# A tuned encoder layer: weight sums in DRAM given out in another order

## The chip, the cores and the metric

The kernel runs on one core of one Trainium2 chip. The metric is the device time of one execution in microseconds (us). Three runs of the kernel before took 811.58, 812.87 and 814.30 us; their median is 812.87 us. The core has a matmul engine (TensorE, PE in the profile), a vector engine (VectorE, DVE), a scalar engine (ScalarE, ACT), GpSimd (POOL) and SyncE (SP). They run on their own and wait for one another through semaphores. Transfers between DRAM and on-chip memory go over 16 DMA engines; in this kernel SP issues the loads, and POOL issues the transfers that add to what is at their target.

## The reference

One layer of a streaming encoder over 512 frames with 1024 channels, in float32:

```python
u = rmsnorm(h, g_mix)
proj = u @ w_in      # GLA q,k,v,out-gate,low rank | FoX q,k,v,forget | memory query | 3 branch gates
# branch A: gated linear attention in chunks of 64 frames, normed, times silu(out-gate), @ w_gla_o
# branch B: forgetting attention (8 heads, causal), @ w_fox_o
# branch C: cross attention into rmsnorm(mem) @ w_mem_kv (4 heads), @ w_mem_o
gt = sigmoid(gates)
merged = gt[0] * y_gla + gt[1] * y_fox + gt[2] * y_mem
h = h + merged @ w_out
u2 = rmsnorm(h, g_ffn)
h = h + square(relu(u2 @ w_ff1)) @ w_ff2
out = rmsnorm(h, g_final)
```

The large products are u by w_in (1024 by 6680), merged by w_out, and the feed-forward block (1024 by 4096 and back).

## The kernel before, in words

**Products.** Every float32 weight chunk of 512 KB is loaded into a tile `raw`, and *split*: ScalarE casts it to a shortened float type (`hi`, or `whi`), VectorE subtracts that from the load (`lo`, or `wlo`). Three products, hi by hi, hi by lo and lo by hi, then make one (`mm3`, L186 to L188). The ring of `raw` tiles has three buffers, and so have the rings of `hi` and `lo`: a load starts when the third split before it is done.

**Seven products instead of eight.** The GLA value and out-gate columns of w_in, the branch gates and w_ff1 and w_ff2 are multiplied in 2 by 2 blocks by a scheme that needs seven block products and, in return, sums of blocks. Sums of activations are made by VectorE. Sums of weights are made by DMA: a transfer copies a block in DRAM to a scratch tensor in DRAM, and later ones, issued by POOL, add other blocks to it. The scratch tensors are G1 to G4 for the GLA columns (`gsum`, 1 MB each) and T1 to T4 for w_ff1 (`tsum`). The ff block runs over four quarters of w_ff1. The first quarter has tensors of 512 KB (T1 to T4, in two halves, numbered 0 and 4); each of the later quarters, 1 to 3, has T1 and T3 of 1 MB. The gates' sums are made in on-chip memory instead (`wb`, L1211, POOL too), and so are most later ones of the ff block (`b`, L1855, and `tq`, L1572).

**What sets the pace of the sums in DRAM.** `next_sum` (L136) is called at every split, from `split_w` (L173) and, in the gate products, from `high` (L1222). After the first seven splits it takes the next entry of a list, if there is one, and issues that transfer on POOL so that it waits for the cast of this split. An add waits, besides, for the transfer that wrote its target before. There are two lists: `first_ops()` (G1 to G4, then the first quarter's T1 to T4, then T3 of quarters 1 to 3), and T1 of quarters 1 to 3. `late_on` switches from the first to the second, in the round that is named (2, 7) before. The second list's transfers also wait for the last merge of the second branch.

**Order.** The program is written by stages, which overlap: the front (memory keys and values, norm of x); FoX attention, woven with projections and with GLA products 1, 5, 2 and 6 (`linear`, L552); memory attention, woven with the FoX output product and GLA products 7 and 3; GLA, woven with its product 4 and the memory branch's output; then *rounds*, a list of block products of the three branch gates with the merge, `("Y", ...)` for the GLA output product and `("O", ...)` for half of the product with w_out (L1417 to L1440); then the other half of w_out, the second norm and the ff block. PE's order is the written one. The other engines' order inside most stages is set by a scheduler that simulates the program; in the rounds and a few other places it is the written one (`in_order`). All engines take their instructions in order, so one that waits holds back all behind it.

GLA product 4 (`linear(4, A22r)`) reads G4, the ff block's first quarter T4, T3 and the others, and the second quarter T1 and T3 of quarter 1. PE reads a sum only by way of a load and a split.

Of the kernel before, what the change touches and what calls it, by code (L numbers as in the profile page):

```python
# [58 lines left out]
def hybrid_block(ctx, tc, chunks, wst, memT, xT, xN, gffn, gfin, wup, cst, out):  # L59
# [16 lines left out]
    def pool(name, side=None, bufs=1):  # L76
        return tc.tile_pool(name=name, bufs=bufs, side=side, reuse_waits="tile")
# [32 lines left out]
    def linear_ops():  # L110
        for n, src, add in ((1, "11", 0), (3, "12", 0), (1, "12", 1), (2, 1, 0), (2, "22", 1), (3, "22", 1), (4, 2, 0), (4, "21", 1)):
            if isinstance(src, str):
                i = index["N", "w_in", 4 * (src[0] == "2"), OFF["gv" if src[1] == "2" else "gg"]]
                src = wst[i:i + 2]
            else:
                src = gsum[src]
            yield gsum[n], src, add

    def sum_ops(ops, qs):
        for n, src, add in ops:  # L120
            for q in qs:
                i = index["F", q % 4, 0 if q else 1, src] if isinstance(src, str) else None
                yield tsum[n, q], tsum[src, q] if i is None else wst[i:i + (2 if 0 < q < 4 else 1)], add

    def first_ops():
        lin = linear_ops()
        ff = sum_ops(((1, "11", 0), (3, "12", 0), (1, "12", 1), (3, "22", 1), (2, 1, 0), (2, "22", 1), (4, 2, 0), (4, "21", 1)), (0, 4))
        for own, others in ((4, 1), (1, 3), (1, 1), (1, 1), (1, 0)):
            yield from islice(lin, own)
            yield from islice(ff, others)  # L130
        yield from ff
        yield from sum_ops(((3, "12", 0), (3, "22", 1)), (1, 2, 3))

    sums = [first_ops(), sum_ops(((1, "11", 0), (1, "12", 1)), (1, 2, 3))]
    late_on, merged = [], [None]
    chunk_n, cast_now, low_now, hold = [0], [None], [None], [None]  # L136

    def next_sum(after):

        chunk_n[0] += 1  # L140
        if chunk_n[0] <= 7:
            return
        for to, src, add_ in islice(sums[len(late_on)], 1):
            with tc.issue_after(merged[0]) if late_on else ExitStack():
                if add_:
                    d = nc.gpsimd.dma_start(to, src, accum_op=ALU.add, max_dma_last_dim=8192)
                else:
                    d = nc.gpsimd.dma_start(to, src)
            tc.add_manual_dep(d.ins, after.name, mybir.DependencyInfo(mybir.DependencyClass.Sync, mybir.DependencyReason.DATA),
                              reason="pace")  # L150

    @contextmanager
    def in_order(*others):

        engines = (mybir.EngineType.DVE, mybir.EngineType.Activation, mybir.EngineType.SP, *others)
        traced = nc.cur_bb.bb.instructions
        last, behind = traced[-1], {}
        yield
        for i in traced[next(k for k in reversed(range(len(traced))) if traced[k] is last) + 1:]:
            if i.engine in engines:  # L160
                if i.engine in behind:
                    tc.add_manual_dep(i, behind[i.engine].name, mybir.DependencyInfo(
                        mybir.DependencyClass.NoSync, mybir.DependencyReason.DATA), reason="order")
                behind[i.engine] = i
# [53 lines left out]
    def run(*gens):  # L218
        for g in gens:
            for _ in g:  # L220
                pass
# [391 lines left out]
    with pool("fox") as xp:  # L613
# [242 lines left out]
        T, V_, R, A, K = fox_turn, fox_values, fox_rows, fox_scores, fox_masks  # L856
# [54 lines left out]
    with pool("mematt") as ap:  # L911
# [3 lines left out]
        def mem_q(h):  # L915
            def evac(ps):
                st["q", h] = [ap.tile([P, S], F32R, tag=g, name=nm(g), bufs=2) for g in ("qh", "ql")]
                st["low"] = split(*st["q", h], ps)
            return proj(OFF["mq"] + P * h, evac)
# [44 lines left out]
        Q, A, T, V_ = (lambda i: run(mem_q(i))), mem_scores, mem_turn, mem_values  # L964
# [183 lines left out]
    def h_tile(t, name):  # L1148
        return hp.tile([P, D], F32, tag=f"h{t}", name=nm(name))
# [18 lines left out]
    with pool("outp") as op_:  # L1168
# [38 lines left out]
        def load_sum(g, n, other):  # L1207
            nc.sync.dma_start(sum_tile(g, n, other), wst[index[gate_key(GATES[g], "12" if other else "11", n)]])

        def plus(g, n, other, b):  # L1210
            nc.gpsimd.dma_start(sum_tile(g, n, other), wst[index[gate_key(GATES[g], b, n)]], accum_op=ALU.add)  # L1211
# [10 lines left out]
        def high(r, c):  # L1222
            ws[r, c] = pair_tiles()
            next_sum(nc.scalar.copy(ws[r, c][0], source(r, c)).ins)  # L1224

        def low(r, c):
            hi, lo = ws[r, c]
            nc.vector.tensor_tensor(lo, source(r, c), f(hi), op=ALU.subtract)  # L1228
            if r[0] not in ("Y", "O") and r[1] in (1, 5, 6) and r != (0, 1):
                plus(r[0], c, 0, {1: "12", 5: "22", 6: "21"}[r[1]])  # L1230
# [30 lines left out]
        def bend():  # L1261
            for x, to in bent:
                nc.scalar.activation(x, x, AF.Tanh, scale=0.5)
                if to[0] < 2:
                    todo.extend((*to, t) for t in range(2))
            bent.clear()
# [36 lines left out]
        def merge(g, i, c, half):  # L1303
            t = 2 * i + half
            x, a = th[g, i, c][:, half], half_of(acc[t], c)
            if g == 0:
                nc.vector.scalar_tensor_tensor(a, x, 1.0, a, op0=ALU.add, op1=ALU.mult)
            else:
                nc.vector.scalar_tensor_tensor(x, x, 1.0, half_of(ymem[t], c), op0=ALU.add, op1=ALU.mult)
                merged[0] = vec(a, a, x)  # L1310
# [56 lines left out]
        def go(when, i):  # L1367
            for fn, args in when.get(i, []):
                fn(*args)
# [5 lines left out]
        with in_order(mybir.EngineType.Pool):  # L1375
            for n in range(2):
                load_sum(0, n, 0)
                plus(0, n, 0, "12")
            go(loads, 0)
            loads[0] = []  # L1380
            for n in range(2):
                load_sum(0, n, 1)
            for i, r in enumerate(rounds):
                now[0] = r
                if r == (2, 7):
                    omst.close()
                    mhp = late.enter_context(pool("mhl"))
                    mh, ml = (mhp.tile([P, KT, S], F32R, name=x) for x in ("mh", "ml"))
                if r == ("Y", 0):
                    hN += [h_tile(t, "h") for t in range(NT)]  # L1390
                    gf = hp.tile([P, D], F32, tag="gf", name="gf")
                    for t in (2, 3, 0, 1):
                        nc.sync.dma_start(hN[t], xN[t * P:(t + 1) * P, :])
                    nc.sync.dma_start(gf, gffn)
                if r == ("O", 0):
                    mst.close()
                    unp.append(late.enter_context(pool("un")))
                go(loads, i)
                go(early, i)
                n = NT if r[0] in ("Y", "O") else 2  # L1400
                parts, due = todo[:1], [(r2, c) for r2 in rounds[i + 1:i + 2] for c in range(2)]
                del todo[:1]
                for x in parts:
                    merge(*x)
                if i:
                    evac(rounds[i - 1], NT - 1 if rounds[i - 1][0] in ("Y", "O") else 1)
                for t in range(n):
                    mms(r, t)
                    if t == 0:
                        for x in due:  # L1410
                            high(*x)
                            low(*x)
                        bend()
                        go(after, i)
                        if r == (2, 7):
                            late_on.append(1)
                    else:  # L1417
                        evac(r, t - 1)
                    if r == ("Y", 0):
                        turn(t, 1)  # L1420
                    if r == ("O", 1):
                        turn(t, 0)
            evac(r, n - 1)
# [761 lines left out]
```

## Time and profile before

| | |
|---|---|
| median of three runs | 812.87 us |
| the profiled execution | 813.05 us |
| its span, first to last instruction | 811.3 us |
| mean granted PE clock | 0.991 of full speed |
| PE busy | 793.0 us, 98% of the span |
| VectorE, ScalarE, POOL busy | 76%, 58%, 12% |
| DMA moved | 165.44 MB, of it 65.02 MB by POOL's queue (q0) and 95.72 MB by SP's (q1) |
| share of the 16 DMA engines | 38.1% by POOL's queue, 32.8% by SP's |
| sums of T from weights | 12 of 512 KB and 6 of 1 MB with sizes shown, and 6 copies |

The profile is of one execution. Times are in us from the start of the span. L176 is line 176 of the kernel before. `raw<-in_wst_dram` reads "raw written from the weights in DRAM". In a row of the timeline stand start, duration, engine, line, operation, output and inputs, and in brackets the idle time of the engine ahead of it with what ended it. In the view of the chain of waits each row is start, duration and what the time went to: a DMA row runs from its issue to the instruction that it released. A row of the DMA view ends with the time from issue to landing. Ends of products are modelled, so the distance between the starts of two products is the better measure.

In the pages' rows the DRAM tensors are just `T` and `G`; in the rows on order they have numbers, where T_0, T_1 to T_3 and T_4 are the ff quarters (0 and 4 the halves of the first), and G_91 to G_94 are G1 to G4. T_0_77 is T1 and T_0_79 is T3 of the first quarter; T_1_82, T_2_84 and T_3_86 are T3 of the other quarters, T_1_81, T_2_83 and T_3_85 are their T1.

### The profile page before, as it was taken

To read this page: it belongs to the slowest core of one execution; us is meant where nothing else is said; L and a number is where in the kernel's file an instruction comes from. 1 tells how busy PE (TensorE), PEld (TensorE's weight loads), DVE (VectorE), ACT (ScalarE), POOL (GpSimd) and SP (SyncE) were. 2 spreads that over 40 slices of the span, in tenths; PEclk is the share of its full clock that TensorE was granted. 3 is DMA by queue.
4 is the path that set the end of the run, shared out by engine and by line. 5 is a ranking of instruction groups with operands and counts; after the bars stand their busy time and mean duration, and the time that the engine had idled before them with its cause. 6 is when DMAs were issued, how large, how long until landed. Compare 5 with 4: busy or idle time off the path is not lost.

```text
span 811.3 us, 11675 instructions
## 1 busy us (share of the span) xinstructions
PE 793.0 (98%) x4351; PEld 678.6 (84%) x4351; DVE 620.3 (76%) x971; ACT 474.2 (58%) x746; POOL 97.4 (12%) x137
## 2 busy tenths in 40 slices
PE   9999999989999999999999999999999999999995
PEld 7788888868888888788887789987998899889975
DVE  6878899756777677667744748788789778987896
ACT  7767566534554465655622546864676467646854
POOL 0001000110110122202110000012001200110011
PEclk9999999999999999999999899999999999999998
DMA  9354766993869469798879515998967986798453
GB/s 356 138 166 170 243 228 182 268 272 108 230 242 258 149 186 232 201 239 199 204 246 308 161 52 198 283 233 216 233 180 189 222 220 178 179 253 228 99 91 117
DMA packets 41577, 165.44 MB, mean 204 GB/s; under 512 B 4944, under 2 KB 5648, under 8 KB 39440
## 3 DMA queue, kind: packets, MB, share of 16 engines
q0 software_dynamic: 12448, 65.02, 38.1%
q1 hardware_dynamic: 27712, 95.72, 32.8%
q10 hardware_dynamic: 1360, 3.96, 1.5%
q8 instruction: 34, 0.56, 0.3%
q14 instruction: 23, 0.19, 0.1%
HBM read 162.55 MB, written 31.49 MB: 239 GB/s over the span
## 4 chain that ended last, share of the span: by engine, by line
PE 84%; DMA 8%; DVE 5%; issue 1%; ACT 1%; SPq 0%; POOLq 0%; DVEq 0%; POOL 0%; ACTq 0%
PE mm L1465 16%; PE mm L186 14%; PE mm L187 14%; PE mm L188 14%; DMA raw<-in_wst_dram 6%; PE a L188 4%; PE a L186 4%; PE a L187 4%; PE mm L1805 3%; PE mm L1806 1%; DMA xt<-in_xT_dram 1%; PE mm L715 1%; DVE wlo L177 1%; PE a L430 1%; DMA mem_s<-in_memT_dram 1%
## 5 line engine op out<-in xcount | busy, mean ns | idle before, releaser
L177 DVE TENSOR_TENSOR wlo<-raw,whi 128x1024 fp32r<-128x1024 f32 x44 | 53.8, 1223 | 35.7 <-ACT whi L176 35.0
L176 ACT CAST whi<-raw 128x1024 fp32r<-128x1024 f32 x44 | 46.2, 1050 | 53.5 <-DMA raw<-in_wst_dram 18.4
L1465 PE MATMUL mm<-u,hi 128*128 128x256 f32 x384 | 64.7, 283 | 0.0
L1465 PEld LDWEIGHTS mm<-u,hi 128*128 128x128 f32 x384 | 56.4, 189 | 0.1
L187 PE MATMUL mm<-lo,ch 128*128 128x512 f32 (+1 forms) x132 | 51.2, 388 | 0.4 <-DVE lo L1525 0.4
L186 PE MATMUL mm<-hi,ch 128*128 128x512 f32 (+1 forms) x132 | 50.9, 386 | 0.0
L188 PE MATMUL mm<-hi,cl 128*128 128x512 f32 (+1 forms) x132 | 50.9, 386 | 0.0
L1524 ACT CAST hi<-raw 128x1024 fp32r<-128x1024 f32 x34 | 35.7, 1051 | 25.8 <-PE mm L1465 12.2
L1525 DVE TENSOR_TENSOR lo<-raw,hi 128x1024 fp32r<-128x1024 f32 x34 | 41.5, 1222 | 10.3 <-ACT hi L1524 10.3
L1855 POOL DMA_DIRECT2D b<-in_wst_dram x30 | 25.7, 855 | 197.6 <-DVE lo L1525 89.6
L1465 PE MATMUL mm<-u,lo 128*128 128x256 f32 x192 | 47.5, 283 | 0.0
L1465 PE MATMUL mm<-u2s,hi 128*128 128x256 f32 x288 | 47.3, 283 | 0.0
L186 PE MATMUL mm<-uhl,whi 128*128 128x512 f32 x112 | 44.6, 399 | 0.0
L188 PE MATMUL mm<-uhl,wlo 128*128 128x512 f32 x112 | 43.9, 392 | 0.1
L187 PE MATMUL mm<-uhl,whi 128*128 128x512 f32 x112 | 43.7, 390 | 0.0
L1524 ACT CAST hi<-b 128x1024 fp32r<-128x1024 f32 x26 | 27.3, 1048 | 25.7 <-PE mm L188 18.4
L1465 PEld LDWEIGHTS mm<-u2s,hi 128*128 128x128 f32 x288 | 41.5, 190 | 0.0
L1525 DVE TENSOR_TENSOR lo<-b,hi 128x1024 fp32r<-128x1024 f32 x26 | 31.7, 1221 | 7.9 <-ACT hi L1524 7.7
L186 PE MATMUL a<-hi,ch 128*128 128x512 f32 (+1 forms) x96 | 37.1, 387 | 0.4 <-DVE h L1518 0.4
L1228 DVE TENSOR_TENSOR lo<-wb,hi 128x1024 fp32r<-128x1024 f32 x21 | 25.3, 1222 | 15.7 <-ACT hi L1224 15.7
L187 PE MATMUL a<-lo,ch 128*128 128x512 f32 (+1 forms) x96 | 37.1, 387 | 0.0
L188 PE MATMUL a<-hi,cl 128*128 128x512 f32 (+1 forms) x96 | 37.0, 385 | 0.0
(531 smaller groups left out, 2393.7 us busy)
## 6 DMA issues: line engine op xcount, KB each, us to landing
raw<-in_wst_dram SPq DMA_DIRECT2D x108, 512.0 KB
b<-in_wst_dram POOLq DMA_DIRECT2D x32, 512.0 KB, 5.6
wb<-in_wst_dram POOLq DMA_DIRECT2D x24, 512.0 KB, 7.6
b<-in_wst_dram SPq DMA_DIRECT2D x16, 512.0 KB
raw<-T SPq DMA_DIRECT2D x14, 512.0 KB
T<-in_wst_dram POOLq DMA_DIRECT2D x12, 512.0 KB, 6.3
T<-in_wst_dram POOLq DMA_DIRECT2D x6, 1024.0 KB, 11.8
wb<-in_wst_dram SPq DMA_DIRECT2D x12, 512.0 KB
```

The costliest lines, as they stand in the source:

```text
L176: cast = nc.scalar.copy(hi, raw)
L177: low_now[0] = nc.vector.tensor_tensor(lo, raw, f(hi), op=ALU.subtract).ins
L186: nc.tensor.matmul(ps, lh, rh, start=start, stop=False, skip_group_check=on)
L187: nc.tensor.matmul(ps, lh, rl, start=False, stop=False, skip_group_check=on)
L188: nc.tensor.matmul(ps, ll, rh, start=False, stop=stop, skip_group_check=on)
L430: nc.tensor.matmul(ps, x[:, k, sl], w[low][:, kk, :], start=k == low == 0 and x is mxh, stop=k == KT - 1 and low == 1)
L1228: nc.vector.tensor_tensor(lo, source(r, c), f(hi), op=ALU.subtract)
L1465: nc.tensor.matmul(ps[:, a, :], x[:, a, k, :], y[:, s, k, :], start=start, stop=stop, skip_group_check=go is not None)
L1524: split_now[0] = nc.scalar.copy(hi, raw).ins
L1525: split_now[1] = nc.vector.tensor_tensor(lo, raw, f(hi), op=ALU.subtract).ins
L1805: nc.tensor.matmul(ps, wh[:, a, k, :], u[:, k], start=k == 0, stop=False, skip_group_check=True)
L1855: nc.gpsimd.dma_start(to[i], wst[index["B", q, i, x]], accum_op=ALU.add)
```

## The change

The entries of `first_ops()` are given out in another order, which is now written as a string with one letter for each split: L is the next entry for the GLA sums, F the next one for the first ff quarter, T the next one for T3 of quarters 1 to 3, and a dash is a split that gives out nothing. The first ten entries are as before. Then come five splits with nothing, where the adds to T1 of the first quarter, the copy and the add for G4, and an add to T3 stood. G4's copy and add follow, alternating with the three 1 MB copies for T3 of quarters 1 to 3; the three 1 MB adds to them come every third entry. What is left of the first quarter (T4) comes last, so that the list is five splits longer and ends within the GLA stage and the first rounds. The second list, T1 of quarters 1 to 3, is switched on in round (2, 4), two rounds later than (2, 7), with one output product between them. No transfer is added, dropped or resized, and no product, cast or load is.

```diff
     def first_ops():
         lin = linear_ops()
         ff = sum_ops(((1, "11", 0), (3, "12", 0), (1, "12", 1), (3, "22", 1), (2, 1, 0), (2, "22", 1), (4, 2, 0), (4, "21", 1)), (0, 4))
-        for own, others in ((4, 1), (1, 3), (1, 1), (1, 1), (1, 0)):
-            yield from islice(lin, own)
-            yield from islice(ff, others)
+        third = sum_ops(((3, "12", 0), (3, "22", 1)), (1, 2, 3))
+        for who in "LLLLFLFFFL-----LTLTTFFTFFTFFT":
+            yield from islice({"L": lin, "F": ff, "T": third}[who], 1) if who != "-" else [None]
         yield from ff
-        yield from sum_ops(((3, "12", 0), (3, "22", 1)), (1, 2, 3))
...
-        for to, src, add_ in islice(sums[len(late_on)], 1):
+        for to, src, add_ in filter(None, islice(sums[len(late_on)], 1)):
...
-                        if r == (2, 7):
+                        if r == (2, 4):
                             late_on.append(1)
```

## The prediction

> **What bounds the kernel now.** I read the page first, then TensorE's (PE's) waits, then a table of stretches, then the chain of waits inside the two stretches where PE loses time. The page's span:
>
> ```profile
> span 811.3 us, 11675 instructions
> ```
>
> The profiled execution took 813.05 us, so 1.75 us lie outside the span; it stands 0.18 us above the median of the runs shown (812.87). PE is busy nearly throughout, so a change of DMA order can only pay where PE waits. The view of PE's waits (total, times, longest, in us) has three that touch this change:
>
> ```profile
> PE a L186 <- ACT mh L1322: 2.6, 1, 2.6
> PE a L186 <- ACT qh L239: 1.9, 1, 1.9
> PE a L188 <- DVE ql L240: 1.0, 1, 1.0
> ```
>
> The table of stretches says where, and what the DMA engines did then (us of each engine with its count, then the granted PE clock, the busy share of the 16 DMA engines, GB/s):
>
> ```profile
> 144.00:183.00 39.00, 35.99 (x171) 29.89 (x170) 24.46 (x31) 17.52 (x26) 6.31 (x9) 0.96 0.98 269
> 205.00:224.00 19.00, 19.00 (x105) 16.37 (x104) 16.54 (x26) 9.90 (x20) 3.42 (x5) 1.00 0.90 260
> 224.00:231.00 7.00, 7.00 (x33) 5.79 (x32) 5.38 (x13) 6.10 (x15) 0.48 (x1) 1.00 0.12 46
> 420.00:445.00 25.00, 25.00 (x127) 20.60 (x126) 10.00 (x14) 4.46 (x7) 1.62 (x2) 1.00 1.02 292
> 445.00:463.00 18.00, 15.25 (x55) 11.74 (x54) 11.37 (x16) 10.92 (x17) 0.00 (x0) 0.81 0.52 172
> 463.00:488.00 25.00, 25.00 (x129) 21.16 (x129) 14.82 (x24) 11.49 (x24) 1.65 (x3) 1.00 0.20 64
> ```
>
> Both gaps end a stretch in which the DMA engines are full (0.98, 1.02), and in both the clock falls (0.96, 0.81). The chain of waits (start, duration) names the late thing, weight loads:
>
> ```profile
> 147.58 14.17 DMA raw<-in_wst_dram
> ...
> 164.17 10.98 DMA raw<-in_wst_dram
> ```
>
> ```profile
> 422.63 23.68 DMA raw<-in_wst_dram
> ```
>
> Why PE feels a late load shows on ScalarE, which runs in order: a cast that waits for its load (the load of 164.17, there at 175.2; the one below) holds back the evacuation that stands behind it, qh in the first gap (A, at 175 us) and mh in the second (B, at 445).
>
> ```profile
> 176.18 0.58 ACT L239 CAST qh<-mm 128x512 fp32r<-128x512 f32 x1
> ```
>
> ```profile
> 445.13 1.04 ACT L1224 CAST hi<-raw 128x1024 fp32r<-128x1024 f32 x1 [11.93 <-DMA raw<-in_wst_dram]
> ```
>
> **Gap A (175 us), the first term.** Price it from PE's own rows: the last product of the second memory query, and the first of the third.
>
> ```profile
> 174.54 0.39 PE L188 MATMUL mm<-uhl,wlo 128*128 128x512 f32 x1
> ...
> 183.79 0.39 PE L186 MATMUL mm<-uhl,whi 128*128 128x512 f32 x1
> ```
>
> Between them stand 12 score products and 12 output products. Undisturbed, 12 score products take 1.43 us (208.12 to 209.55), and a 512-column product follows the last in 0.227 us (459.66 to 462.38 holds 12):
>
> ```profile
> 208.12 0.28 PE L186 MATMUL a<-mkh,qh 128*128 128x256 f32 x1
> ...
> 209.55 0.40 PE L186 MATMUL mm<-whi,s 128*128 128x512 f32 x1
> ```
>
> ```profile
> 459.66 0.39 PE L186 MATMUL a<-hi,mh 128*128 128x512 f32 x1
> ...
> 462.38 0.39 PE L186 MATMUL mm<-f0h,mh 128*128 128x512 f32 x1
> ```
>
> So the third query could start at 174.54 + 0.23 + 1.43 + 12 x 0.227 = 178.92 us and starts at 183.79: A costs 4.9 us, 2.9 of waiting and 2.0 of slow clock.
>
> What the change does there: five casts in a row give out no sum. These are the issues that go, first and last of five:
>
> ```profile
> 146.59 0.79 POOL L146 DMA_DIRECT2D T<-in_wst_dram  x1 [1.35 <-ACT whi L176]
> ...
> 167.06 0.79 POOL L146 DMA_DIRECT2D T<-in_wst_dram  x1 [3.08 <-ACT whi L176]
> ```
>
> They are three adds of 512 KB, one copy of 1 MB and one add of 1 MB. Lone DMAs (issue to landing in us, last number) land in:
>
> ```profile
> T<-in_wst_dram POOLq DMA_DIRECT2D x1, 512.0 KB, 5.5
> ```
>
> ```profile
> T<-T POOLq DMA_DIRECT2D x1, 512.0 KB, 3.8
> ```
>
> ```profile
> T<-in_wst_dram POOLq DMA_DIRECT2D x1, 5.5
> ```
>
> ```profile
> G<-in_wst_dram POOLq DMA_DIRECT2D x1, 1024.0 KB, 8.4
> ```
>
> in order a 512 KB add, a 512 KB copy, a 1 MB copy (its size is not printed) and a 1 MB add. Steps between these rows price the DMA work: another 512 KB of adding is 8.4 - 5.5 = 2.9 us, of copying 5.5 - 3.8 = 1.7. The five are then 5 x 2.9 + 2 x 1.7 = 18 us of DMA time out of a stretch of 39 that is full. To save A, the load that came at 175.2 must come by about 172; the two loads in its chain took 14.17 and 10.98 us. With 18 us of work gone from around them I expect more than these 3. ScalarE's order here is unchanged, and the second-next bound, the cast's target buffer, comes free when PE ends the first query, at about 169 us. **I take the whole 4.9 us**; bounds 0 (the load still later than 175) and 4.9.
>
> **Gap B (445 us), the second term.** Last transposes at 444.78, then the round's 48 products, then the next product at 462.38 (above).
>
> ```profile
> 444.78 0.60 PE L1320 MATMUL mm<-cst_s,acc 128*128 128x128 f32 x4
> ```
>
> Undisturbed: 444.78 + 0.60 + 48 x 0.227 = 456.28, so B costs 6.1 us, 2.6 of waiting and 3.5 of slow clock. The load of 422.63 stood behind five 512 KB loads and these six sums (first and last):
>
> ```profile
> 403.53 0.54 POOL L148 DMA_DIRECT2D T<-in_wst_dram  x1 [11.54 <-ACT hi L1224]
> ...
> 429.82 0.80 POOL L146 DMA_DIRECT2D T<-in_wst_dram  x1 [7.35 <-ACT f0h L1224]
> ```
>
> Three are copies, three adds of 1 MB. T1's list now opens two rounds later, so before the load lands only two copies stay, on the casts at 420 and 428: an add at 415.77 and two at 421.65 and 429.82 leave, 3 x 2 x 2.9 = 17 us of adding, and one copy with them. The load needs to be some 4 us earlier (cast, cast, evacuation before 445.4). **I take the whole 6.1 us**; bounds 0 and 6.1.
>
> Where T1's work goes: its last copy and three adds fall on 436 to 460 us, by the casts of the last product and of its successor. In the table 445 to 463 is half empty and 463 to 488 four fifths; its 6 x 2.9 + 2 x 1.7 = 21 us fit into 18 x 0.48 + 25 x 0.80 = 28.6 us idle. If that cover were gone, the weights for the ff block's first products would come late and each us would be PE's. The sums themselves are read a quarter later. On ScalarE and VectorE, in the same place, two casts and subtractions move behind one evacuation (ACT, where the last product's weights are cast; mh is the merged activation turned for it). Before:
>
> ```order
> 360 L1322 ACTIVATE mh<-mm_4146 128x4x128
> 361 L239 CAST f1h_4261<-raw_4263 128x1024
> 362 L239 CAST f0h_4255<-raw_4257 128x1024
> 363 L176 CAST whi_4269<-raw_4267 128x1024
> 364 L1322 ACTIVATE mh<-mm_4165 128x4x128
> 365 L1155 ACTIVATE hsq_4204,hss_3028<-h_3971 128x512
> ```
>
> of the change:
>
> ```order
> 360 L1321 ACTIVATE mh<-mm_4144 128x4x128
> 361 L238 CAST f0h_4253<-raw_4255 128x1024
> 362 L1321 ACTIVATE mh<-mm_4163 128x4x128
> 363 L238 CAST f1h_4259<-raw_4261 128x1024
> 364 L175 CAST whi_4267<-raw_4265 128x1024
> 365 L1154 ACTIVATE hsq_4202,hss_3028<-h_3967 128x512
> ```
>
> The evacuation comes earlier and the two casts one step later, some 10 us ahead of their products: nothing, with the 48 products as cover. Loads (SP) and products (PE) keep their order.
>
> **Memory stage (205 us), the third term, a loss.** The sums that left 146 to 168 come back here. POOL gives out the sums, one row each (G: the GLA weights' sums; T with a quarter: the ff weights'; 64x2048 is an add of 512 KB, 128x2048 of 1 MB; 16 rows are a copy). From the 1 MB add near 144 us on, before:
>
> ```order
> 23 L146 DMA G_93<-in_wst_dram 128x2048
> 24 L146 DMA T_0_77<-in_wst_dram 64x2048
> 25 L148 DMA G_94<-G_92 16x16384
> 26 L146 DMA T_4_87<-in_wst_dram 64x2048
> 27 L146 DMA G_94<-in_wst_dram 128x2048
> 28 L146 DMA T_0_79<-in_wst_dram 64x2048
> ```
>
> of the change:
>
> ```order
> 24 L147 DMA G_94<-G_92 16x16384
> 25 L147 DMA T_1_82<-in_wst_dram 16x16384
> 26 L145 DMA G_94<-in_wst_dram 128x2048
> 27 L147 DMA T_2_84<-in_wst_dram 16x16384
> 28 L147 DMA T_3_86<-in_wst_dram 16x16384
> 29 L145 DMA T_0_77<-in_wst_dram 64x2048
> 30 L145 DMA T_4_87<-in_wst_dram 64x2048
> 31 L145 DMA T_1_82<-in_wst_dram 128x2048
> ```
>
> G4 and the 1 MB copies of T3 of quarters 1 to 3 have come ahead of the adds for the first ones, each at least a memory-stage cast later than its row's old place. The tight spot is one load and what its cast holds back: the exponentials of the third head (L939), behind which VectorE scales them (L943) and PE turns them (L951).
>
> ```profile
> 213.03 1.05 ACT L176 CAST whi<-raw 128x1024 fp32r<-128x1024 f32 x1 [3.86 <-DMA raw<-in_wst_dram]
> ```
>
> That load meets, in place of an add of 512 KB, a 1 MB copy (5.5 against 5.5 us, no difference) and then, in place of a copy of 512 KB, an add (5.5 - 3.8 = 1.7 more); the next pair is the same again. Later by 0 (it passes before the second DMA) to 3.4 us; a gain is excluded, as PE has no gap to return in that stretch (19.00 of 19.00). A gap of 3.4 would bring a slow spell like B's, 3.5: bounds 0 and 6.9. **I take 1.0 us**, the half of the first pair and a little, without a clock loss. [...] After it, the extra adding (1.7 + 1.7 + 2.9) fills the 6.2 us that 224 to 231 has idle. G4's add now issues near 182 and waits on POOL for G4's copy, two casts before it, with only sums behind; it has until these loads:
>
> ```profile
> 231.51 2.12 SPq L566 DMA_DIRECT2D raw<-G  x2
> ```
>
>
> **GLA stage.** From 231 on there are 512 KB sums where 1 MB ones were, less to move, and five more sums behind them. On POOL they now stand around the powers that the GLA norms need; what could be late is the third power, behind an add that follows the cast at 278.88:
>
> ```profile
> 278.88 1.04 ACT L176 CAST whi<-raw 128x1024 fp32r<-128x1024 f32 x1
> ```
>
> ```profile
> 283.32 1.01 POOL L1107 TENSOR_TENSOR stat<-stat,mhalf 128x4 f32<-128x4 f32 x1 [10.93 <-DVE stat L1106]
> ```
>
> The add would issue at about 280.2 and be off POOL at 281.0, 2.3 us before the power's operand. Nothing; if later, each us goes to the turns behind the norm.
>
> **Sum.** 813.05 - 4.9 - 6.1 + 1.0 = 803.05 us for a profiled execution; 0.18 less for a median of runs: **802.9 us**.
>
> **Rivals.** (1) One cure is lost or given back. For it: ScalarE's blocked order stays as it was, and A's and B's loads still share with 1 MB sums. Against it: both stretches lose 18 us of DMA time and more. Only B cured: 802.9 + 4.9 = 807.8; only A: 809.0; both cured but the full 6.9 at 213 us: 808.8. (2) Only the waits return and the slow spells stay: 812.87 - 1.9 - 1.0 - 2.6 + 1.0 = 808.4. The row against it: the clock is 1.00 in every stretch above but the two with gaps. [...] (3) Slower: the backlog of 144 to 183 moves whole into the memory stage, whose casts block ScalarE in the same way. Price: 18 us of waiting and two slow spells of 3.5, less 11.0: +14, 827 us; it decides where the casts from 213.03 on come over 7.5 us late in sum (7.5 and one spell of 3.5 eat 11.0). Against it: 224 to 231 is idle to 88%. (4) The change does nothing measurable, since gains and new gaps cancel or the loads wait for buffers instead: 812.9.
>
> **Chances.** Forecast (800 to 805.5) 0.70; (1) 0.14; (2) 0.03; (3) 0.05; (4) 0.05; below 800, by a gain that I don't see, 0.03. I call faster what is over 0.3% (2.4 us) below 812.87, about what a measurement of this kernel tells from no change. (1) and (2) are faster: 0.90; same 0.05; slower 0.05. The range goes from 800 (third term 0, and runs 1.3 us under their median, as the fastest shown) to 809 (the bound of the third term, and one cure lost).
>
> **What would show it.** A right: the waits on qh and ql leave PE's list, the clock is 1.00 in 144 to 183, and the third query's first product follows the second's last within 4.5 us, not 9.25. B right: the wait on mh at L1322 is gone and the last product's loads take 12 us, not 23. Third term: a new wait of PE at L951 in the third head's turn, about 1 us. Wrong: a slow clock anywhere between 180 and 300 us, or ScalarE waiting over 5 us for raw there.

## The result, and the profile after

The changed kernel took 800.10, 800.70 and 803.69 us; the ratio to the kernel before, which ran beside it, is 0.986, with a 95% interval of 0.982 to 0.990. (A fourth run took 1595.49 us, of a cause that nothing here shows; the ratio leaves it out.) Four more runs of it, in the experiments, had a median of 803.34 us (801.91 to 807.28) and a ratio of 0.987 (0.983 to 0.991). The forecast was 802.9. The profiled execution took 800.10 us. Its page begins:

```profile
span 798.3 us, 11673 instructions
```

The span is 13.0 us shorter. Line numbers are one less than in the kernel before. The view of PE's waits no longer has qh, ql or mh; its longest rows are:

```profile
PE a L327 <- DVE warm L324: 1.2, 1, 1.2
PE mm L185 <- ACT hi L1223: 0.6, 1, 0.6
```

The stretches of the table shown of before (PE, weight loads, VectorE, ScalarE and POOL busy, then the granted clock, the DMA share, GB/s):

```profile
144.00:183.00 39.00, 39.00 (x194) 33.07 (x193) 29.82 (x42) 20.49 (x36) 2.67 (x4) 1.00 0.79 233
205.00:224.00 19.00, 19.00 (x95) 16.03 (x94) 15.09 (x30) 10.50 (x27) 1.61 (x2) 1.00 0.99 260
224.00:231.00 7.00, 7.00 (x36) 5.90 (x35) 5.54 (x8) 4.52 (x6) 2.12 (x3) 1.00 0.56 138
420.00:445.00 25.00, 25.00 (x125) 20.70 (x124) 13.83 (x18) 7.96 (x11) 1.34 (x2) 1.00 0.81 268
445.00:463.00 18.00, 18.00 (x81) 14.90 (x80) 9.85 (x16) 7.95 (x15) 2.19 (x3) 1.00 0.92 250
```

The clock is 1.00 in both places that had a gap, and the DMA engines went from 0.98 to 0.79 (A) and from 1.02 to 0.81 (B). The work is now in 205 to 224 (0.90 before, 0.99 now), 224 to 231 (0.12, now 0.56) and 445 to 463 (0.52, now 0.92), and PE does not feel it there. The timeline of PE at the two places, the last product of the second memory query and the first of the third, then the last transposes of the round and the first product of the next:

```profile
174.01 0.39 PE L187 MATMUL mm<-uhl,wlo 128*128 128x512 f32 x1
...
178.42 0.39 PE L185 MATMUL mm<-uhl,whi 128*128 128x512 f32 x1
...
438.97 0.60 PE L1319 MATMUL mm<-cst_s,acc 128*128 128x128 f32 x4
...
450.32 0.39 PE L185 MATMUL mm<-f0h,mh 128*128 128x512 f32 x1
```

The first distance fell from 9.25 to 4.41 us, the second from 17.60 to 11.35: 4.84 and 6.25 us. The forecast took 4.9 and 6.1. On ScalarE the casts ahead of the two evacuations now have their loads in time, so that qh follows at 170.0 us (176.2 before) and mh at 432.8 (447.3 before):

```profile
169.04 1.03 ACT L175 CAST whi<-raw 128x1024 fp32r<-128x1024 f32 x1
169.99 0.57 ACT L238 CAST qh<-mm 128x512 fp32r<-128x512 f32 x1
```

```profile
431.83 1.05 ACT L1223 CAST hi<-raw 128x1024 fp32r<-128x1024 f32 x1 [0.23 <-DMA raw<-in_wst_dram]
432.79 1.07 ACT L1321 ACTIVATE mh<-mm 128x512 fp32r<-128x512 f32 x2
```

Of the 13.0 us, 1.9 are left: 0.4 from the small waits for weights just ahead of A, 0.4 at 320 us, where PE's wait on `hi` fell from 1.0 to 0.6, 0.9 at 530 to 550, and 0.2 elsewhere. The second profile of the changed kernel, with a span of 800.4, lost 0.6 and 1.6 us again at 320 and at 530 to 550, so what was gained there in the first is no more than scatter.

### The profile page after: what moved, and what is told of

Read it like the earlier page. It is cut to its first block, busy times and chain, and to the rows that moved or that the text cites. A ratio compares the mean times of both kernels' runs of the same rounds, so it can differ in the third digit from the quotient of the medians.

```text
span 798.3 us, 11673 instructions
## 1 busy us (share of the span) xinstructions
PE 786.9 (99%) x4351; PEld 675.8 (85%) x4351; DVE 620.5 (78%) x971; ACT 474.2 (59%) x746; POOL 97.5 (12%) x137
## 4 chain that ended last, share of the span: by engine, by line
PE 94%; DVE 3%; ACT 1%; issue 1%; DMA 1%; POOLq 0%; DVEq 0%; POOL 0%; ACTq 0%
PE mm L185 16%; PE mm L186 16%; PE mm L187 16%; PE mm L1464 16%; PE a L185 5%; PE a L186 5%; PE a L187 5%; PE mm L1804 3%; PE mm L416 1%; PE mm L1805 1%; PE a L429 1%; PE mm L714 1%; PE a L770 1%; DVE lo L1904 1%; PE a L809 1%; PE a L808 1%
```

## The experiments

Each edit stands against the changed kernel, unless the text names another. Kernels that were timed together share their runs of the kernel before; the ratio, with its 95% interval, is what is compared. A load's landing is the time of the last increment of the semaphore that its cast waits for. Some expectations give the end of a load's last packet instead, counted in the order of the queue; for the loads that they name that is 0.3 to 3.2 us earlier.

### One half of the change alone

```diff
-        for who in "LLLLFLFFFL-----LTLTTFFTFFTFFT":
+        for who in "LLLLFLFFFLFLFLFFFFFFFFFFTTTTTT":
```

> The first list stands in its old order, without empty splits; only the second list opens in round (2, 4) as changed. Theory (each gap has its own DMA cause, A the sums of 146 to 168 us, B those of 415 to 430 us): gap A is as before, with PE's waits on qh (about 1.9 us) and ql (1.0) and a clock below 1.00 in 144 to 183; gap B is gone. The changed kernel's three runs had about 800.7, so 800.7 + 4.9 = 805.6 us, 0.991 of before. Rival 1 (the sums that pile up after the first list, and not T1's place, made B late): B stays too, 812. Rival 2 (the late switch does everything): 801.

Measured: 808.64 us, 0.993 (0.991 to 0.995), 3 us above the theory's time: A itself costs 4.3 us, but PE also loses 1.4 us just ahead of it and 1.1 at 520 to 560. A is back and B is gone. The waits, and the two stretches (columns as above):

```profile
PE a L185 <- ACT qh L238: 1.2, 1, 1.2
...
PE a L187 <- DVE ql L239: 1.0, 1, 1.0
```

```profile
144.00:183.00 39.00, 36.12 (x170) 29.41 (x169) 23.88 (x30) 17.51 (x26) 6.30 (x9) 0.96 0.97 265
445.00:463.00 18.00, 18.00 (x83) 14.97 (x82) 9.30 (x13) 8.53 (x13) 1.63 (x2) 1.00 0.90 233
```

```diff
-                        if r == (2, 4):
+                        if r == (2, 7):
```

> The first list in its new order with the five empty splits, the second list opened in round (2, 7) as before. Theory: A is gone, B is back with PE's wait on mh (2.6 us) and the slow clock behind it: 800.7 + 6.1 = 806.8 us, 0.992 of before. Rival (B was the tail of a state that A left, such as the clock or a queue's backlog): 801.

Measured: 807.81 us, 0.992 (0.988 to 0.995). A is gone and B is back, with PE's first products behind the wait now 0.43 us apart instead of 0.23:

```profile
PE a L185 <- ACT mh L1321: 2.3, 1, 2.3
```

```profile
443.68 0.77 PE L187 MATMUL a<-hi,ml 128*128 128x512 f32 x1 [0.63 <-DVE ml L1322]
444.25 0.63 PE L185 MATMUL a<-hi,mh 128*128 128x512 f32 x1
444.67 0.63 PE L186 MATMUL a<-lo,mh 128*128 128x512 f32 x1
```

The rivals of both fall. The halves act apart: 0.69% and 0.84% make 1.5%, and the whole has 1.4%.

### The empty splits and the order behind them

```diff
-        for who in "LLLLFLFFFL-----LTLTTFFTFFTFFT":
+        for who in "LLLLFLFFFLLTLTTFFTFFTFFT":
```

> The changed kernel without its five empty splits, with the same new order of letters. In 146 to 168 us then stand G4's copy and add and three copies of 1 MB, by the prediction's prices 2 x 2.9 + 8 x 1.7 = 19.4 us of DMA time against 18 before. Theory (any DMA work of that size makes the load late): A is back, 4.9 us (3 to 6): 805.6. Rival (it is the adds, which read and write their target, and the 512 KB ones above all; copies share well): 0 to 1.5 us, 801 to 802.

Measured: 813.59 us, 1.000 (0.998 to 1.002): all of the gain is lost, more than A was worth. PE waits at two places, first for the weights of the second query (161 us), then for qh:

```profile
PE a L185 <- ACT qh L238: 3.2, 1, 3.2
PE mm L185 <- ACT whi L175: 1.5, 1, 1.5
```

The theory gave 4.9 us (3 to 6) at A; it lost 4.4 us before 172 us and 6.2 behind. The rival, that copies share well, is refuted the other way round: three 1 MB copies in the place of three adds of 512 KB made it worse.

```diff
-        for who in "LLLLFLFFFL-----LTLTTFFTFFTFFT":
+        for who in "LLLLFLFFFL-----FLFLFFFFFFFFFFTTTTTT":
```

> The five empty splits, but behind them the old order: the adds to T1 and T3 of the first ff quarter around G4, then the rest of that quarter, the copies and adds of 1 MB for quarters 1 to 3 last. Theory (the empty splits are the cure of A; the order behind them is worth nothing, as the memory stage has no gap): as the changed kernel, 801, within 1 us. Rival (the new order is needed, because the sums that pile up would press on the memory stage or 1 MB sums on the GLA stage): 803 to 806, with a wait of PE in 205 to 320 us.

Measured: 813.31 us, 1.000 (0.997 to 1.002). The theory fell. A is gone as it should, and a new wait of 9.9 us has come at 304 us, the largest of all:

```profile
PE mm L185 <- ACT ct L1283: 9.9, 1, 9.9
```

The chain of waits names a load again, and POOL's timeline what it met: the list, now five splits longer, ends in adds of 1 MB where the changed kernel has a copy and two adds of 512 KB.

```profile
291.63 18.74 DMA raw<-in_wst_dram
```

```profile
273.01 0.91 POOL L145 DMA_DIRECT2D T<-in_wst_dram  x1 [6.03 <-ACT whi L175]
274.83 0.82 POOL L145 DMA_DIRECT2D T<-in_wst_dram  x1 [0.92 <-ACT whi L175]
...
287.52 0.84 POOL L145 DMA_DIRECT2D T<-in_wst_dram  x1 [4.47 <-ACT whi L175]
```

The load of 291.6 us landed 18.7 us behind its issue here and 6.1 in the changed kernel. The evacuation of `ct` stands behind its cast on ScalarE, as qh did in A. So the empty splits alone are worth nothing: they push the pile into the next place without slack, where 11.3 us are lost. The order behind them, which brings the 1 MB sums forward into the memory stage, is as much of the cure as they are.

```diff
-        for who in "LLLLFLFFFL-----LTLTTFFTFFTFFT":
+        for who in "LLLLFLFFFL-----LTLTTTTTFFF":
```

> The changed kernel with the three adds of 1 MB for T3 of quarters 1 to 3 on three casts in a row, right behind their copies, and the rest of the first quarter behind them; the empty splits stay. Against the changed kernel some 2 x 2.9 = 5.8 us more adding stands ahead of the loads of 202 to 209 us, which took 9.4 to 12.5 us there without a wait of PE. Theory (a pile of 1 MB adds makes loads late wherever it stands, and the memory stage is near its bound): a gap in 205 to 231 with a slow clock, 803 to 808, most likely 805. Rival (only their lateness mattered, that they end before the loads of 274 to 294 us, not their spacing): 801.

Measured: 802.69 us, 0.987 (0.985 to 0.989), as the changed kernel. The rival holds: the spacing of the adds is worth nothing. The memory stage is full to its end,

```profile
205.00:224.00 19.00, 19.00 (x95) 16.04 (x94) 14.02 (x25) 9.20 (x24) 1.65 (x3) 1.00 1.04 256
224.00:231.00 7.00, 7.00 (x37) 5.88 (x36) 5.75 (x11) 5.62 (x10) 1.56 (x2) 1.00 1.01 247
```

and a load issued at 209.2 us landed 17.9 us later (13.3 in the changed kernel, 8.2 in the kernel before), without a wait of PE. This stage has slack: full DMA engines and late loads cost nothing in it.

### The DMA work by itself

In two kernels each empty split gives out a copy, from the weights to a scratch tensor that nothing reads, of 512 KB (`n = 1`) or 1 MB (`n = 2`):

```diff
+        extra = ((dram.tile([n, P, 1024], F32, name=f"X{k}"), wst[at0:at0 + n], 0) for k in range(5))
...
-            yield from islice({"L": lin, "F": ff, "T": third}[who], 1) if who != "-" else [None]
+            yield from islice({"L": lin, "F": ff, "T": third, "-": extra}[who], 1)
```

> The changed kernel with a copy of 512 KB, from the weights to a scratch tensor that nothing reads, at each of the five empty splits: by the prediction's price 5 x 1.7 = 8.5 us of DMA time put back of the 18 that left. The load that blocked ScalarE ended at 173.9 us in the kernel before and at 165.6 in the changed one, where about 172 is early enough, so some 5 us are in hand. Theory (a threshold: a later load costs nothing until its cast blocks an evacuation): the load comes some 4 us later and PE does not wait, 801 us. Rival (the loss grows with the DMA work): half of A, 803.3.

Measured: 803.67 us, 0.988 (0.986 to 0.991). The time alone can't tell the theory from the rival, since the changed kernel itself had a median of 803.34 in its later runs. The profile can: PE has no wait on qh or ql and loses nothing at A, with the DMA engines at 0.91:

```profile
144.00:183.00 39.00, 39.00 (x192) 32.65 (x192) 29.50 (x42) 21.66 (x36) 5.11 (x9) 1.00 0.91 285
```

> The same with five copies of 1 MB: 5 x 2 x 1.7 = 17 us, nearly what left. Nothing else is moved against the changed kernel up to here, so this is the DMA work alone. Theory: the load is late again, with a wait of PE on qh or on the products ahead of it and a slow clock behind it: A is back, 805.5 (803.5 to 812, since 1 MB copies cost more than priced where the empty splits were taken out). Rival (what cured A is what the new order put last, or POOL's own order): 801.

Measured: 812.31 us, 0.996 (0.994 to 0.998). A is back, and larger than with the five sums:

```profile
PE a L187 <- ACT qh L240: 2.9, 1, 2.9
PE mm L187 <- ACT whi L177: 1.5, 1, 1.5
```

```profile
144.00:183.00 39.00, 32.92 (x156) 26.62 (x155) 22.84 (x29) 18.03 (x26) 5.09 (x9) 0.98 0.95 323
183.00:205.00 22.00, 22.00 (x102) 18.65 (x101) 13.56 (x26) 9.47 (x25) 0.52 (x2) 0.88 0.56 168
```

So transfers alone, with every other instruction in its place, make the gap. The threshold theory holds, and its price does not: 17 us by the prediction's prices were to cost 4.9 us and cost 10, 3.0 before 172 us and 7.1 at A. The packets of the two traces in 144 to 183 give other prices. A copy of 1 MB is 16 packets of 64 KB, of 2.4 us (before) to 2.9 us (changed kernel) in the mean, as many as there are engines; an add of 1 MB is 128 packets of 8 KB, of 0.68 us before, 128 x 0.68 / 16 = 5.4 us. The five copies keep the engines 5 x 2.7 = 13.5 us, the five sums of before 3 x 2.7 + 5.4 + 2.4 = 16 us, and the lighter set does more harm. The next kernel has the same copies in packets of 8 KB:

```diff
-                    d = nc.gpsimd.dma_start(to, src)
+                    small_ = {"max_dma_last_dim": 8192} if any(to is x for x in extra_to) else {}
+                    d = nc.gpsimd.dma_start(to, src, **small_)
```

> The kernel with five scratch copies of 1 MB at the empty splits, with each copy cut into packets of 8 KB (128 of them) in place of 16 packets of 64 KB; the same bytes at the same places. With 64 KB packets these copies lost 10 us at 160 to 188 us, more than the 5 us of the five sums of the kernel before, though the packets kept the 16 engines only 5 x 2.7 = 13 us against 16. Theory 1 (a load waits behind whole packets, so a long packet weighs more than its share): less is lost, 3 to 7 us, so 805 to 809, and loads of 146 to 168 us land earlier. Theory 2 (the bytes moved decide): 812, as with long packets. If 8 KB packets are slower by the byte (an add's take 0.68 us each, 5.4 for 1 MB), it may come out slower than that.

Measured: 804.26 us, 0.988 (0.985 to 0.991). The waits left at A, and the stretch:

```profile
PE a L193 <- DVE ql L245: 1.0, 1, 1.0
...
PE a L191 <- ACT qh L244: 0.3, 1, 0.3
```

```profile
144.00:183.00 39.00, 37.72 (x185) 31.27 (x184) 26.49 (x35) 18.32 (x28) 5.28 (x9) 1.00 0.97 333
```

The same bytes, the engines as busy (0.97 and 0.95), and 2 us lost in place of 10: less is lost, as Theory 1 has it, and less than the 3 to 7 us that it gave. The short packets are not slower by the byte: in this stretch POOL's queue moved 8.43 MB in 949 packets in 64.0% of the engines' time, and with long ones 8.39 MB in 368 packets in 64.9%. The copies themselves land later, 10.8 us where the long ones took 8.3 (each kernel's view of DMA issues in 144 to 183):

```profile
X<-in_wst_dram POOLq DMA_DIRECT2D x5, 1024.0 KB, 10.8
```

```profile
X<-in_wst_dram POOLq DMA_DIRECT2D x5, 8.3
```

Loads have packets of 4 KB, of 0.18 us each in the kernel before. Theory 1's reason, that a load waits behind whole packets, is the author's guess: which packet an engine takes next is not in the records. These two runs show the loss, and the load of the cast ahead of qh landing at 173.5 us in place of 179.3.

Beside each other, for the load of the cast ahead of qh (PE's loss is the time that PE needed for the same products, less the changed kernel's: from the product at 155 us of the changed kernel to that at 172, and from there to that at 190):

| kernel | the load's landing, us | PE lost before 172 us | and at A |
|---|---|---|---|
| the changed kernel | 165.9 | 0.0 | 0.0 |
| copies of 512 KB | 171.2 | 0.3 | 0.0 |
| copies of 1 MB in packets of 8 KB | 173.5 | 0.0 | 2.1 |
| the kernel before | 175.2 | 0.4 | 4.8 |
| old order, late switch | 175.4 | 1.4 | 4.3 |
| copies of 1 MB | 179.3 | 3.0 | 7.1 |
| no empty splits | 179.4 | 4.4 | 6.2 |

Up to 171.2 us a load that lands 5 us later costs nothing at A; from 173.5 on each costs. In the kernel with no empty splits ScalarE is held longest one cast earlier: that load landed at 177.1 us, after a wait of 11.1.

### What the second list does in B, and the floor

```diff
-                        if r == (2, 4):
+                        if r == (2, 7):
...
                 if add_:
+                    if late_on: continue
```

> The kernel with the new string and the old switch (2, 7), with the three copies of 1 MB of its second list but without its three adds (T1 of quarters 1 to 3 then lacks a block, so the output is not the reference's). By the packets of the trace the three adds are 3 x 128 x 0.64 / 16 = 15 us of the 16 engines in 403 to 445. Theory (B is these adds): B is gone, 6 us below the kernel with them (807.8), so as the changed kernel. Rival (the four loads of h, gf and the copies are enough to hold the weights back): B stays, 806 to 808.

Measured: 803.36 us, 0.986 (0.982 to 0.989): B is gone, with no wait on mh and a DMA share of 0.60:

```profile
420.00:445.00 25.00, 25.00 (x125) 20.63 (x124) 17.33 (x23) 9.36 (x13) 0.00 (x0) 1.00 0.60 218
```

The three adds make B, through the loads of h that stand before the weights on SP's queue: these four landed 16.3 to 23.4 us behind their issue with the adds (16.8 to 23.7 in the kernel before), 6.4 to 9.2 without them, and 4.6 to 13.8 in the changed kernel, where the adds come later.

```diff
-        for to, src, add_ in filter(None, islice(sums[len(late_on)], 1)):
+        for to, src, add_ in ():
...
-                src = gsum[{5: 1, 6: 2, 7: 3, 4: 4}[n]][c]
+                src = wst[c]
...
-            return tsum[n, q][i] if q else tsum[n, 0 if i else 4][0]
+            return wst[i]
...
-                nc.sync.dma_start(tq[i], tsum[1, q][i])
+                nc.sync.dma_start(tq[i], wst[i])
```

> All copies and adds of both lists are left out, and the loads that read them read plain weights of the same size instead, so the numbers are not the reference's; everything else is as changed. This is the floor for any order of these sums. Theory (the changed kernel has no gap left that the sums make): as the changed kernel in the same rounds, within 1.5 us. Rival (their share of the DMA engines still costs in many small places): 3 to 6 us faster than it.

Measured: 800.82 us, 0.983 (0.980 to 0.987), where the changed kernel, timed beside it, had 803.34. With a DMA share of 0.40 in place of 0.79 at A,

```profile
144.00:183.00 39.00, 39.00 (x194) 33.06 (x193) 30.03 (x42) 20.84 (x36) 0.00 (x0) 1.00 0.40 133
```

PE's waits have nearly the same rows, none over 1.2 us. The two intervals overlap, and the difference of 2.5 us lies between the theory's 1.5 and the rival's 3, so neither is decided. More than about that is not to be had from the order of these sums.

The changed kernel was run again as it is:

> The changed kernel as it is, for more runs beside the others. Theory: 0.986 of before (0.982 to 0.990), no wait on qh, ql or mh. If the loss of some 1 us at 530 to 545 us, which the other kernels have and its first profile had not, is a matter of its DMA phase and not of the change, it may show up here too.

Measured: 803.34 us, 0.987 (0.983 to 0.991), no wait on qh, ql or mh. The loss at 530 to 550 us was there, 1.6 us. Over all kernels it lies between nothing and 2.4 us against the first profile of the changed kernel, and 1.6 on the same kernel again; what makes it is open.

### The clock

On the kernel with B (string new, switch old):

```diff
                     if r == ("O", 1):
                         turn(t, 0)
+                        if t == NT - 1:
+                            for _ in range(12):
+                                nc.tensor.matmul(wide["O", 1][0], mh[:, 5, :P], mh[:, 4], start=False, stop=False, skip_group_check=True)
```

> The kernel with the new string and the old switch (2, 7), which has gap B, with twelve products more (they add something wrong to one output tile) between the last transposes and the product that waits for mh, 12 x 0.227 = 2.7 us, as long as the wait of 2.5 us. The load and the evacuation stay as late; only PE is not idle. Theory (the slow clock is a consequence of PE's idle time): the clock stays 1.00 in 420 to 463, products behind stand 0.23 us apart and not 0.43, and the time is some 1.7 us below that kernel's (807.8 in an earlier call). Rival (the clock falls for another reason, or a 0.6 us wait is enough for it): 0.43 apart again, and the time as that kernel's or a little above.

Measured: 805.90 us, 0.990 (0.987 to 0.993), against 0.992 without the filling. The intervals overlap; the profile is clear. Behind the wait, and the stretch:

```profile
445.19 0.50 PE L187 MATMUL a<-hi,ml 128*128 128x512 f32 x1 [0.43 <-DVE ml L1322]
445.53 0.40 PE L185 MATMUL a<-hi,mh 128*128 128x512 f32 x1
445.77 0.40 PE L186 MATMUL a<-lo,mh 128*128 128x512 f32 x1
```

```profile
420.00:445.00 25.00, 24.75 (x123) 20.10 (x121) 11.69 (x16) 6.69 (x10) 0.81 (x1) 1.00 0.92 277
445.00:463.00 18.00, 17.81 (x78) 14.75 (x79) 12.53 (x19) 10.34 (x17) 0.00 (x0) 1.00 0.57 187
```

The products stand 0.23 us apart and the clock is 1.00, though the first evacuation of mh is as late as without the filling, 2.2 us behind the start of the last transposes in both. From the last transposes to the first product of the next stage the loss is 3.5 us in place of 5.0, 2.8 of it the filling. So the slow spell of B is a consequence of PE's idle time.

How much a spell costs is in the granted clock of narrow windows of the kernel before: it is 0.50 from 178.12 to 181.53 us, at A, and 0.50 from 447.77 to 454.60, at B. Half of these 3.4 and 6.8 us is 1.7 and 3.4, near the 2.0 and 3.5 of slow clock that the prediction read off PE's rows.

## Why the prediction was right, and where not

**The sum.** 802.9 us was forecast; three runs with a median of 800.70 and four with 803.34 lie around it, inside the range. Two terms of three were right to 0.2 us. That the sum is so near is luck in part: the third term was 1.0 us too high, and scatter of the same size at 320 and 530 to 550 us stands in none of the terms.

**A, 4.9 us.** Right in size (4.84), place and mechanism. That the load must come by "about 172" is what the table of loads shows (171.2 is enough, 173.5 is not quite), and in the changed kernel it landed 9 us earlier. Its sign that the third query follows within 4.5 us came out as 4.41.

**B, 6.1 us.** Right: 6.25, and the kernel without the three adds shows that they make it. The casts that change places on ScalarE played no part: the evacuations of mh that were late stand ahead of them in both orders. The weights' loads landed 14.9 to 16.2 us behind their issue (16.8 to 24.9 before), not the 12 of the prediction's sign. Ahead of the late one stood seven loads, not five: the four of h, that of gf and two chunks of weights.

**The memory stage, +1.0 us.** Mis-sized: it was nothing, and no run shows the term. The load named as the tight one was issued at 200.81 us and landed 6.2 us later, after 6.8 in the kernel before, so it is the lower bound that held. The 1.7 us by which an add was to hold it up longer than a copy did not come. The copy and the add that it was to meet were issued at 199.8 and 201.4 us; why they did not delay it stays open. Its cast still waits for it,

```profile
207.09 1.05 ACT L175 CAST whi<-raw 128x1024 fp32r<-128x1024 f32 x1 [3.30 <-DMA raw<-in_wst_dram]
```

but PE does not. The loads behind it did come later (10.2, 13.5, 13.3 us for 6.3, 6.0, 8.2) and there was room: with still later ones, in the kernel with adjacent adds, PE lost nothing either. The upper bound of 6.9 us, and rival 3 built on it, took the stage to be as tight as A; it is not.

**The step that was nearly missed.** The prediction laid A's cure on the five empty splits and looked for a later danger at the third power on POOL, finding none. That holds for this change. But with the old order behind the empty splits 11.3 us are lost at 304 us, at the loads of the gates' weights, which the prediction never looked at; its remark that from 231 us on there is "less to move" was the point on which most of the gain hung (11.3 of 13.0 us), and it was priced at nothing.

**The currency.** "18 us of DMA time" was near in total (16 by the packets) but wrong as a measure of harm: a copy of 512 KB, priced at 1.7 us, occupies 1.4, and five copies of 1 MB, 13.5 us of the engines, did more harm than the five sums of 16. In packets an eighth as long they did less.

**The rivals.** (1) did not come: A and B are apart and neither was given back. (2), waits without their slow spells, did not come either: the spells went with the waits, and the filled gap shows why: with PE idle for 0.4 us the clock stayed 1.00 in 420 to 463, and with PE idle for 2.9 us it was 0.97 in 420 to 445 and 0.94 in 445 to 463 (string new, switch old). How long a wait brings a spell the runs do not settle: waits of 1.2 and 1.0 us within 2.7 us brought 0.96 over 39 us (old order, late switch), and 0.3 and 1.0 brought none (copies in packets of 8 KB). (3), the backlog moved whole into the memory stage, failed since PE lost nothing there. (4), nothing, fell with the ratio.

## What to carry to other kernels

In this kernel background transfers cost nothing until one load missed the moment at which its cast blocks ScalarE, and from there on they cost the wait (at A nothing with the load at 171.2 us, 2.1 us with it at 173.5) and, with the load at 175.2 us or later, a slow clock too (0.96 over 144 to 183 in the kernel before). So find that moment for each stage, and give out no transfers that the loads before it must share with. Taking work out of a full stretch is half of a cure; look where the list ends now, and at every load there that has an evacuation standing behind its cast. Where background copies must share with loads, try short packets: 8 KB in place of 64 KB saved 8 us here.

## What was not expected of the hardware

At the same bytes and nearly the same share of the engines the length of packets decided: five 1 MB copies in packets of 64 KB cost PE 10 us at a DMA share of 0.95, and in packets of 8 KB 2 us at 0.97. The 1 MB copies of the changed kernel itself (G4's and those of T) still have packets of 64 KB; shorter ones there were not tried.
